# Moving R21's second-level differences one or two pairs earlier in both SwiGLUs of a macaron retention block

## The chip, the core and the metric

The kernel runs on one core of a Trainium2 chip. The metric is the time of one execution on the device, in microseconds (us), as the median of several runs; smaller is better. The engines are named as in the profile: PE is TensorE (matmuls), PEld its weight loads, DVE is VectorE, ACT is ScalarE, SP is SyncE, which issues the DMAs.

## The reference

One encoder layer over 1024 tokens of width 1024, in float32:

```python
h = h + 0.5 * swiglu_ffn(rmsnorm(h, norm_ffn1), ffn1_w_in, ffn1_w_out)
u = rmsnorm(h, norm_mix); proj = u @ w_in                 # q, k, v, gates, pool input
...                                                       # retention, pooling, gated merge
h = h + merged @ w_out
h = h + 0.5 * swiglu_ffn(rmsnorm(h, norm_ffn2), ffn2_w_in, ffn2_w_out)
return rmsnorm(h, norm_final)

def swiglu_ffn(x, w_in, w_out):                           # D_FF = 2816
    gate, up = jnp.split(x @ w_in, 2, axis=-1)
    return (jax.nn.silu(gate) * up) @ w_out
```

The case is about the two products `x @ w_in` (1024 x 1024 by 1024 x 5632), one in each SwiGLU.

## The kernel before, in words

**Three matmuls for one.** Every float32 operand is held as two halves, a rounded one and the rest. `split` makes them: ACT casts the first half (line 158), DVE subtracts to get the second (line 159). `mm3` (lines 178 to 180) then does three matmuls for each product of two blocks. The weights pass through `weights`, into a ring of five buffers (`wt`).

**Groups.** `w_in` is worked off in 22 groups, each of one 128-column tile of the gate and one of up. A group is one Strassen (Winograd) step over 2 x 2 blocks, with seven products, each of 12 matmuls of 128 x 512. `strassen` returns them as a list of steps (prepare, multiply): index 0 is P1 = L11 R11, 1 is P6 = S2 T2, 2 is P5 = S1 T1, 3 is P7 = S3 T3, 4 is P2 = L12 R21, 5 is P3 = S4 R22, 6 is P4 = L22 T4. L are weights; the S are sums of them, made by DVE for each group (lines 439, 452 and 456). R and T belong to the tokens and are made once for the whole SwiGLU, each in four tiles.

**Products in common.** `common(nx, A, B, n)` does P2 (n = 2) or P3 (n = 3) of two groups A and B together by a further Strassen step, in 42 matmuls of 128 x 256 instead of 24 of 128 x 512. It wants four differences of the token operand (y1 to y4 of R21 or of R22), which `Next.blocks` makes once, in six pieces of work: lines 356 (sums), 364 (differences), 158 and 159 (their splits). y1 is written over a block of the operand that the common product does not use, so from then on no plain P2 (or P3) may follow. A common product is three steps; its weights need one split of 128 x 512 and one of 128 x 256 more than the plain pair (`wx`, two `ws`, `wy`), and sums at lines 539, 540, 546 and 547; its results are put together by copies on ACT and additions on DVE (lines 573, 584, and 722 in `evac`).

**The order.** `pairs_of_both` yields the steps of a SwiGLU. The first two groups go plain (in SwiGLU 1 a third one, and ahead of them group 0 in another form). The others follow in pairs A, B, counted by k = 0, 1, ...: nine pairs in SwiGLU 1 and ten in SwiGLU 2. All of them have P3 in common. Pairs with k < `some` have P2 plain (steps A[4], B[4] right behind A[0], B[0]); with the last of them, k = `some` - 1, R21's differences are put on the queue. From k = `some` on P2 is in common: late in the pair for k = `some`, early in it after that. R22's differences are put on the queue with the last step ahead of the pairs, so that they are made in k = 0.

**The queue.** `Flow.run` prepares (`step[0]`) four steps ahead of the products (`step[1]`), and after each step's products takes one piece of work from a queue, first in, first out:

```python
            ahead.append(step)
            if len(ahead) > LOOK:
                done = ahead.popleft()
                if done is not None:
                    done[1]()
                    self.some(self.rate)
```

`rate` is 1 in both SwiGLUs. The end of a group puts four pieces there (line 736 or 739 multiplies the gate by the norm, ACT applies SiLU, line 742 twice multiplies gate and up), that of every second group four more (lines 755 to 767: operands for the second product, and their stores): 12 for a pair. Where a common product comes to its differences and they aren't made, `flow.until` takes from the queue until they are. What stands in the text in this way is the order of preference; a planner (Tile) that knows the dependences and a time for each instruction writes the final order of each engine's queue from it. Evacuations of PSUM are marked to go first (`soon`).

**Buffers.** The differences that stay live lie in tags `tl` (four buffers: three for R21, one for R22) and `t4` (nine: two for R22, one for the norm, six for the gate and up tiles). `c2` has eight buffers for sums and partial results.

Of the kernel before, what the change touches and what calls it, by code (L numbers as in the profile page):

```python
# [53 lines left out]
BY_OPERAND = (0, 4, 1, 3, 2, 6, 5)  # L54
# [36 lines left out]
def block_kernel(ctx: ExitStack, tc, x, x_tok, vecs, f1_in, f1_out, w_in, w_v, pool_w, w_ret, w_pool, w_o,  # L91
# [34 lines left out]
    def c2(name):  # L126
        return sb.tile([P, H], F32, tag="c2", bufs=N_C2, name=name)
# [8 lines left out]
    def load(dst, src):  # L136
        nc.sync.dma_start(dst, src)
# [8 lines left out]
    def half(t, j):  # L146
        return t[:, j * H : (j + 1) * H]
# [119 lines left out]
    class Next(Norm):  # L267
# [22 lines left out]
        def g(self, mt, v=None):  # L290
            if self.gain is None:
                return None
            v = vec if v is None else v
            return v[:, self.gain + mt : self.gain + mt + 1]
# [315 lines left out]
    def then(step, work):  # L610


        def body():
            step[1]()
            flow.add(*work)

        return step[0], body

    def pairs_of_both(nx, groups, first, some):

        groups = list(groups)
        A, B = (g(()) for g in groups[:2])
        steps = [g[m] for m in first for g in (A, B)]
        n = 2
        if len(groups) % 2:
            C = groups[n](())
            steps += [C[m] for m in BY_SUM]
            n += 1
        tl_, t4_ = ("tl", N_TL), ("t4", N_T4)

        steps[-1] = then(steps[-1], nx.blocks("R22", [t4_, tl_, t4_], True))
        yield from steps
        for k, n in enumerate(range(n, len(groups), 2)):
            A, B = (g((2, 3) if k >= some else (3,)) for g in groups[n : n + 2])
            yield A[0]
            yield B[0]
            if k < some:
                yield A[4]
                yield then(B[4], nx.blocks("R21", [tl_] * 3, True)) if k == some - 1 else B[4]
            elif k > some:  # L640
                yield from common(nx, A, B, 2)

            yield from (A[3], A[1], B[3], B[1], A[2], B[2])
            if k != some:
                yield from common(nx, A, B, 3)
                yield A[6]
                yield B[6]
            else:
                yield from common(nx, A, B, 2)
                yield A[6]  # L650
                yield B[6]
                yield from common(nx, A, B, 3)
# [49 lines left out]
    def ffn_in(nx, w, ops, name, start=None):  # L702

        R, T, B, T4 = ops
        hid = {}

        def group(g):
            gate_up = {}

            def dest(which):  # L710
                tile, j = which
                if tile not in gate_up:
                    gate_up[tile] = (tl if start and g == 0 else t4)(f"{name}{'gu'[tile]}{g}")
                return half(gate_up[tile], j)

            later = []

            def evac(which, in0, in1):
                tile, j = which
                dst, rms = dest(which), nx.rb  # L720
                if in1 is not None:
                    tt(dst, in0, in1, ADD)
                elif not tile and rms is not None:
                    tt(dst, in0, half(rms, j), MUL)
                    return
                else:
                    copy(dst, in0)
                if not tile:
                    later.append(j)

            def end():
                gate, up = gate_up[0], gate_up[1]

                def scale():
                    if len(later) == 2:
                        tt(gate, gate, nx.rms(), MUL)
                    else:
                        for j in later:
                            tt(half(gate, j), half(gate, j), half(nx.rms(), j), MUL)

                def times(j):
                    tt(half(up, j), half(gate, j), half(up, j), MUL)

                flow.add(scale, lambda: act(gate, gate, AF.Silu), lambda: times(0), lambda: times(1))
                hid[g] = up
                k = g % FH
                if g < FH:
                    return
                lo, hi, e = hid.pop(k), up, {}
                R11, R12, R21, R22 = half(lo, 0), half(lo, 1), half(hi, 0), half(hi, 1)  # L750

                def w1():

                    e["n"], e["m"] = gate, c2(f"{name}m{k}")
                    tt(half(e["n"], 0), R12, R11, SUB)

                def w1b():
                    tt(half(e["n"], 1), R22, R12, SUB)
                    load(B[k], e["n"])

                def w2():
                    tt(R12, R22, half(e["n"], 0), SUB)
                    load(R[k], lo)
                    load(T[k], hi)

                def w3():
                    tt(e["m"], R21, R12, SUB)
                    load(T4[k], e["m"])
                    done.add(k)

                flow.add(w1, w1b, w2, w3)

            if start and g == 0:
                return plain_group(nx, start, f"{name}{g}_", evac, end)
            return lambda shared: strassen(nx, w[g, 0], w[g, 1], f"{name}{g}_", evac, end, shared=shared, dest=dest)

        done = ops_done.setdefault(name, set())
        order = [g for k in range(FH) for g in (k, k + FH)]
        if start:

            return chain(group(0), pairs_of_both(nx, (group(g) for g in order[1:]), BY_OPERAND, 3))
        return pairs_of_both(nx, (group(g) for g in order), BY_OPERAND, 2)


    def plain_group(nx, blocks, name, evac, end):

        t, w = {}, {}

        def step(o, i, j):


            def prep():
                if j == 0:
                    w[o, i] = weights(blocks[2 * o + i], f"{name}w{o}{i}")

            def body():
                if i == 0:
                    t[o] = bank(f"{name}{o}{j}")
                for k in range(4):
                    mm3(t[o], parts(w[o, i], k), parts(nx.operand(("R11", "R12", "R21", "R22")[2 * i + j], k)),  # L800
                        i == 0 and k == 0, i == 1 and k == 3)
                if i == 1:
                    evac((o, j), t[o], None)
                    if (o, j) == (1, 1):
                        end()

            return prep, body

        return [step(o, i, j) for j in range(2) for i in range(2) for o in range(2)]
# [285 lines left out]
    def ffn1():  # L1095
        for n, step in enumerate(ffn_in(first, f1_in, ops1, "a", lead)):
            flow.rate = 1
            yield step
        flow.rate = 2
        yield from ffn_out(first, ops1, ops_done["a"], f1_out, x, "b", mix.quarter, end1)  # L1100
# [237 lines left out]
    order = [("q", 0), ("k", 0), *(o for pair in zip(heavy, light) for o in pair), *light[len(heavy) :]]  # L1338
# [482 lines left out]
    def second():  # L1821
        for n, step in enumerate(ffn_in(ffn2, f2_in, ops2, "c")):
            flow.rate = 1
            yield step
        flow.rate = 2
# [89 lines left out]
```

## Time and profile before

| | |
|---|---|
| median of 3 runs (lowest to highest) | 2153.55 us (2153.22 to 2153.73) |
| the profiled execution, its span | 2153.71 us, 2151.9 us |
| granted clock of TensorE | 1.000 |
| PE, PEld, DVE, ACT busy | 2136.8, 1814.0, 1884.0, 1110.4 us |
| SwiGLU 1's pairs, k = 0 to 8 | 87.7 to 424.0 us of the span |
| SwiGLU 2's pairs, k = 0 to 9 | from 1557.2 us of the span |

Rows of the windows view give a stretch, its length, and the busy time and number of instructions (in brackets) of PE, PEld, DVE, ACT and POOL in it, then the granted clock. Rows of the timeline give start, duration, engine, line, operation, output<-inputs, shape and count. A name such as `a_wS` is that of a tile with its numbers left out: a and c are SwiGLU 1 and 2, `a_wL` and `a_wS` are split weights of a plain product, `a_wx`, `a_ws`, `a_wy` those of a product in common, `n1x`, `n1R21y` and `n1R22y` belong to the differences.

### The profile page before, as it was taken

The numbers are of one execution on the slowest core, as the hardware profiler recorded it, in microseconds if no ns is written. First come the engines' busy times: TensorE is split into PE (matmuls) and PEld (weight loads), VectorE is DVE, ScalarE is ACT, GpSimd is POOL, SyncE is SP. The second block draws the span as 40 slices with busy tenths as digits, with TensorE's granted clock in tenths as the row PEclk, the third lists the DMA queues.
The fourth block names the chain that finished last, engine by engine and source line by source line (L and its number), as shares of the span: only waits on it lengthen the run. The fifth ranks groups of instructions, "written<-read, shape, count | busy, mean of one in ns | idle before, by whom it ended". The sixth has DMA issues, their size and how long they took to land.

```text
span 2151.9 us, 30188 instructions
## 1 busy us (share of the span) xinstructions
PE 2136.8 (99%) x10830; PEld 1814.0 (84%) x10830; DVE 1884.0 (88%) x3344; ACT 1110.4 (52%) x2102; POOL 0.2 (0%) x4
## 2 busy tenths in 40 slices
PE   9999999999999999999999999999999999999998
PEld 7888888888888888888888898888888888888887
DVE  8798888997987799999999877899988878899796
ACT  8544444454653544455457753446644544445454
POOL 0000000000000000000000000000000000000000
PEclk9999999999999999999999999999999999999999
DMA  7232423585537333232337567624133242358642
GB/s 255 77 133 74 136 85 128 180 288 183 178 119 245 109 110 123 101 131 105 119 109 242 179 225 251 219 92 162 64 104 116 74 136 85 127 181 292 197 130 100
DMA packets 120135, 320.96 MB, mean 149 GB/s; under 512 B 13232, under 2 KB 17456, under 8 KB 119984
## 3 DMA queue, kind: packets, MB, share of 16 engines
q1 hardware_dynamic: 119408, 317.98, 43.6%
q8 instruction: 85, 1.39, 0.3%
q10 hardware_dynamic: 576, 1.05, 0.1%
q14 instruction: 66, 0.54, 0.1%
HBM read 228.27 MB, written 90.70 MB: 148 GB/s over the span
## 4 chain that ended last, share of the span: by engine, by line
PE 83%; DVE 11%; DMA 2%; ACT 2%; issue 2%; SPq 0%; DVEq 0%; ACTq 0%
PE c_b L178 2%; PE c_b L179 2%; PE c_b L180 2%; PE a_b L178 2%; PE a_b L180 2%; PE a_b L179 2%; PE c_e L178 2%; PE c_e L179 2%; PE c_e L180 2%; PE a_e L179 2%; PE a_e L180 2%; PE a_e L178 2%; PE a_a L180 1%; PE a_a L179 1%; PE a_a L178 1%
## 5 line engine op out<-in xcount | busy, mean ns | idle before, releaser
L179 PE MATMUL c_b<-n3T,c_wS 128*128 128x512 f32 x176 | 68.5, 389 | 0.0
L180 PE MATMUL c_b<-n3T,c_wS 128*128 128x512 f32 x176 | 68.5, 389 | 0.0
L178 PE MATMUL c_b<-n3T,c_wS 128*128 128x512 f32 x176 | 68.2, 389 | 0.0
L178 PE MATMUL a_b<-n1T,a_wS 128*128 128x512 f32 x168 | 65.4, 389 | 0.0
L179 PE MATMUL a_b<-n1T,a_wS 128*128 128x512 f32 x168 | 65.4, 389 | 0.0
L180 PE MATMUL a_b<-n1T,a_wS 128*128 128x512 f32 x168 | 65.3, 389 | 0.0
L179 PE MATMUL a_a<-n1R,a_wL 128*128 128x512 f32 x120 | 46.7, 389 | 0.0
L180 PE MATMUL a_a<-n1R,a_wL 128*128 128x512 f32 x120 | 46.7, 389 | 0.0
L178 PE MATMUL a_a<-n1R,a_wL 128*128 128x512 f32 x120 | 46.7, 389 | 0.0
L179 PE MATMUL c_a<-n3R,c_wL 128*128 128x512 f32 x112 | 43.7, 390 | 0.0
L180 PE MATMUL c_a<-n3R,c_wL 128*128 128x512 f32 x112 | 43.6, 389 | 0.0
L178 PE MATMUL c_a<-n3R,c_wL 128*128 128x512 f32 x112 | 43.6, 389 | 0.0
L178 PEld LDWEIGHTS c_b<-n3T,c_wS 128*128 128x128 f32 x176 | 33.0, 188 | 6.9
L180 PEld LDWEIGHTS c_b<-n3T,c_wS 128*128 128x128 f32 x176 | 33.0, 188 | 6.8
L179 PEld LDWEIGHTS c_b<-n3T,c_wS 128*128 128x128 f32 x176 | 33.0, 188 | 6.8
L179 PEld LDWEIGHTS a_b<-n1T,a_wS 128*128 128x128 f32 x168 | 31.5, 188 | 6.6
L180 PEld LDWEIGHTS a_b<-n1T,a_wS 128*128 128x128 f32 x168 | 31.5, 188 | 6.5
L178 PEld LDWEIGHTS a_b<-n1T,a_wS 128*128 128x128 f32 x168 | 31.5, 188 | 6.5
L159 DVE TENSOR_TENSOR a_wS<-a_S,a_wS 128x512 fp32r<-128x512 f32 x45 | 30.8, 685 | 6.8 <-ACT a_wS L158 6.8
L159 DVE TENSOR_TENSOR c_wS<-c_S,c_wS 128x512 fp32r<-128x512 f32 x46 | 31.5, 684 | 3.7 <-ACT c_wS L158 3.6
L179 PE MATMUL c_e<-n3T,c_wL 128*128 128x512 f32 x88 | 34.4, 391 | 0.0
L178 PE MATMUL c_e<-n3T,c_wS 128*128 128x512 f32 x88 | 34.4, 391 | 0.0
(3380 smaller groups left out, 8178.7 us busy)
## 6 DMA issues: line engine op xcount, KB each, us to landing
c_ra<-in_f_in SPq DMA_DIRECT2D x22, 512.0 KB, 3.7
c_rb<-in_f_in SPq DMA_DIRECT2D x22, 512.0 KB, 4.3
a_ra<-in_f_in SPq DMA_DIRECT2D x21, 512.0 KB, 3.7
a_rb<-in_f_in SPq DMA_DIRECT2D x21, 512.0 KB, 4.3
t<-au SPq DMA_DIRECT2D x11, 512.0 KB, 4.1
b<-ag SPq DMA_DIRECT2D x11, 512.0 KB, 3.5
r<-au SPq DMA_DIRECT2D x11, 512.0 KB, 3.6
br<-r SPq DMA_DIRECT2D x11, 512.0 KB, 5.2
```

The source lines that it names most:

```text
L159: tt(lo, src, hi.bitcast(F32), SUB)
L178: mm(dst, w[0], m[0], start=start, stop=False, skip_group_check=True)
L179: mm(dst, w[0], m[1], start=False, stop=False, skip_group_check=True)
L180: mm(dst, w[1], m[0], start=False, stop=stop, skip_group_check=True)
```

## The change

`pairs_of_both` gets `some` = 1 from both callers, instead of 3 in SwiGLU 1 and 2 in SwiGLU 2. With that R21's differences are put on the queue in k = 0, behind B[4] of that pair, and P2 is in common in k = 1 to 8 of SwiGLU 1 (it was 3 to 8) and in k = 1 to 9 of SwiGLU 2 (it was 2 to 9). Nothing else differs.

```diff
         if start:
 
-            return chain(group(0), pairs_of_both(nx, (group(g) for g in order[1:]), BY_OPERAND, 3))
-        return pairs_of_both(nx, (group(g) for g in order), BY_OPERAND, 2)
+            return chain(group(0), pairs_of_both(nx, (group(g) for g in order[1:]), BY_OPERAND, 1))
+        return pairs_of_both(nx, (group(g) for g in order), BY_OPERAND, 1)
```

## The prediction

> **What bounds the kernel now.** I read the page's busy times and its chain first, then the windows view over single pairs, then the timeline of DVE and PE at the pairs that the change touches.
>
> ```profile
> PE 2136.8 (99%) x10830; PEld 1814.0 (84%) x10830; DVE 1884.0 (88%) x3344; ACT 1110.4 (52%) x2102; POOL 0.2 (0%) x4
> PE 83%; DVE 11%; DMA 2%; ACT 2%; issue 2%; SPq 0%; DVEq 0%; ACTq 0%
> ```
>
> PE is busy for 2136.8 of 2151.9 us and carries 83% of the chain. So a matmul less is time less, and anything else costs only where PE is left without weights. DVE, second with 88%, is the engine that can do that: every product needs a split of its weights, which DVE ends. I call reserve the time from the end of that split to the product's first matmul; as long as it is positive, PE doesn't wait.
>
> The pairs, each from the first matmul of A[0] to that of the next pair's (SwiGLU 1: k = 2, k = 3, k = 4 to 8; SwiGLU 2: k = 1, k = 2):
>
> ```profile
> 163.49:200.94 37.45, 37.45 (x187) 31.82 (x186) 30.64 (x58) 15.36 (x29) 0.00 (x0) 1.00 0.30 106
> 200.94:237.99 37.05, 37.05 (x205) 32.27 (x204) 34.06 (x67) 19.56 (x36) 0.00 (x0) 1.00 0.34 107
> 237.99:424.03 186.04, 185.63 (x1022) 161.25 (x1021) 160.75 (x284) 89.21 (x166) 0.00 (x0) 1.00 0.37 126
> ...
> 1595.34:1632.81 37.47, 37.47 (x188) 31.82 (x187) 34.72 (x65) 17.05 (x32) 0.00 (x0) 1.00 0.30 106
> 1632.81:1669.82 37.01, 37.01 (x205) 32.26 (x204) 33.98 (x67) 19.55 (x36) 0.00 (x0) 1.00 0.32 107
> ...
> 168.93:174.37 5.44, 5.44 (x25) 4.51 (x24) 5.44 (x10) 1.73 (x3) 0.00 (x0) 1.00 0.74 288
> 243.47:248.25 4.78, 4.78 (x43) 4.77 (x42) 4.78 (x9) 4.07 (x8) 0.00 (x0) 1.00 0.00 0
> 88.53:146.00 57.47, 57.43 (x272) 47.62 (x272) 56.94 (x102) 30.41 (x53) 0.00 (x0) 1.00 0.37 129
> 1580.00:1613.80 33.80, 33.75 (x169) 28.29 (x168) 33.00 (x64) 16.56 (x32) 0.00 (x0) 1.00 0.26 84
> ```
>
> PE has no gap in any of them. A pair with P2 plain takes 37.45 or 37.47 us, one with P2 in common 37.05 or 37.01, the later ones 186.04 / 5 = 37.21. The sixth and seventh rows are a plain P2 of two groups (24 matmuls, 5.44 us) and one in common (42, 4.78 us). The last two rows are where the change lands: from before k = 0 until well into k = 1 DVE is full, 56.94 of 57.47 us in SwiGLU 1 and 33.00 of 33.80 in SwiGLU 2. There R22's differences are already being made.
>
> **The change part by part.** *Products.* Three pairs get P2 in common: k = 1 and 2 of SwiGLU 1, k = 1 of SwiGLU 2. PE alone would save 5.44 - 4.78 = 0.66 us for each. The pairs of before show less, since something small comes back in waits. For the form that k = 1 gets, 37.45 - 37.05 = 0.40 and 37.47 - 37.01 = 0.46; for that of k = 2, 37.45 - 37.21 = 0.24. Sum -1.1 us; bounds -2.0 (all of it) and 0.
>
> The Trainium skill has a rule against this ("TensorE: Matmul & The Clock Gate", section "Back-to-back issue gap"): sustained pairs of weight load and matmul are spaced about 131 ns at 512 columns and 81 ns at 128, so narrow matmuls pay for more than their columns. With 98 ns at 256 columns, an estimate between those two, three products in common would lose 3 x (42 x 98 - 24 x 131) = 2.9 us instead of saving. The sixth and seventh rows contradict it, with 5.44 / 24 = 227 ns and 4.78 / 42 = 114 ns, so the sum goes by them.
>
> *DVE's work.* Prices are the pitch at which DVE takes instructions in a run:
>
> ```profile
> 1560.28 1.89 DVE L742 TENSOR_TENSOR cu<-cg,cu 128x512 f32<-128x512 f32 x3
> 118.05 0.75 DVE L159 TENSOR_TENSOR n1R22y<-n1x,n1R22y 128x256 fp32r<-128x256 f32 x2
> 90.27 2.35 DVE L736 TENSOR_TENSOR ag<-ag,n1rb 128x1024 f32<-128x1024 f32 x2
> L356 DVE TENSOR_TENSOR n1x<-n1R 128x512 f32<-128x512 f32 x8 | 5.5, 684 | 0.0
> L159 DVE TENSOR_TENSOR n1R21y<-n1x,n1R21y 128x256 fp32r<-128x256 f32 x6 | 2.5, 419 | 0.0
> ```
>
> Three at 128 x 512 take 1.89 us and one 0.684, so the pitch is 0.60; at 128 x 256 it is 0.75 - 0.419 = 0.33, and at 128 x 1024 about 2.35 / 2 = 1.17. R21's differences are half of the eight sums shown (R22 has the other half), eight differences and eight splits: 4 x 0.60 + 16 x 0.33 = 7.7 us in six pieces of 1.86, 0.66, 1.32, 1.86, 0.66 and 1.32. They exist before too, in k = 2 and k = 1, where no row above shows PE waiting, so nothing is gained by their going. A P2 in common costs DVE three splits of 0.60 and one of 0.33, six narrow sums (2.0), two wide ones (1.2) and two multiplications of 1.17: 7.7 us. Plain it is two splits, two evacuations and two multiplications of 0.60: 3.6. So 4.1 us more for each of the three pairs. Its added casts and copies are ACT's, which is busy for about half of every row above; no DMA is added, and SP's and POOL's queues carry the same.
>
> *Place 1: the first products of k = 1.* In order, R21's six pieces are taken behind the three steps of P3 in common of k = 0, then behind A[6], B[6] and A[0] of k = 1: just after R22's, with DVE full. Preparing runs four steps ahead, so the first four pieces, 5.7 us, stand ahead of the weights of A[1] of k = 1, and the first five, 6.4, ahead of those of B[3]. The 12 pieces of the pair before slide back behind them. And A[4], B[4] of k = 1, two long products that are cheap for DVE, are gone from in between, so that A[3] and what follows is wanted 5.44 us earlier. SwiGLU 1, then SwiGLU 2, around A[1] and B[3] of k = 1:
>
> ```profile
> 127.94 0.68 DVE L159 TENSOR_TENSOR a_wL<-a_ra,a_wL 128x512 fp32r<-128x512 f32 x1
> ...
> 129.48 0.68 DVE L739 TENSOR_TENSOR ag<-ag,n1rb 128x512 f32<-128x512 f32 x1
> 130.08 0.68 DVE L159 TENSOR_TENSOR a_wL<-a_ra,a_wL 128x512 fp32r<-128x512 f32 x1
> ...
> 131.29 0.69 DVE L742 TENSOR_TENSOR au<-ag,au 128x512 f32<-128x512 f32 x1
> ...
> 132.50 0.69 DVE L742 TENSOR_TENSOR au<-ag,au 128x512 f32<-128x512 f32 x1
> ...
> 133.70 0.68 DVE L159 TENSOR_TENSOR a_wS<-a_S,a_wS 128x512 fp32r<-128x512 f32 x1
> 139.57 0.39 PE L178 MATMUL a_b<-n1T,a_wS 128*128 128x512 f32 x1
> 1604.93 0.69 DVE L159 TENSOR_TENSOR c_wS<-c_rb,c_wS 128x512 fp32r<-128x512 f32 x1
> 1611.68 0.39 PE L178 MATMUL c_e<-n3T,c_wS 128*128 128x512 f32 x1
> ```
>
> SwiGLU 1, A[1]: the split ends at 134.38, PE comes at 139.57, reserve 5.2. PE would come 5.44 earlier; DVE has 5.7 more ahead, less the splits of A[4], B[4] (1.2) and the multiplications at 129.48, 131.29 and 132.50 that slide back (1.8): 5.2 - 5.44 - 2.7 = -2.9. SwiGLU 2, B[3]: reserve 1611.68 - 1605.62 = 6.1; less 5.44; 6.4 more ahead, less 1.2, four multiplications (2.4) and one evacuation of A[4] (0.6), so 2.2: -1.5. The other steps between are less negative by the same count. So PE waits 2.9 + 1.5 = 4.4 us in all. DVE being full in those rows, work put ahead delays what follows by its full length, unless the planner puts a sum for a later step behind it: one such sum (0.60) for each place is the nearest thing in those rows. I take 4.4, and keep 0 and 7 as bounds (a reserve off by 2 us either way).
>
> *Place 2: the products in common that follow.* In k = 1 and k = 2 three common products come with only A[6], B[6] and A[0], B[0] between them. SwiGLU 1 before has this at k = 3 and 4, from A[6] of k = 3 to A[3] of k = 4:
>
> ```profile
> 223.56 0.69 DVE L159 TENSOR_TENSOR a_wL<-a_rb,a_wL 128x512 fp32r<-128x512 f32 x1
> 225.67 0.69 DVE L159 TENSOR_TENSOR a_wL<-a_rb,a_wL 128x512 fp32r<-128x512 f32 x1 [1.42 <-ACT a_wL L158]
> 227.57 0.39 PE L178 MATMUL a_e<-n1T,a_wL 128*128 128x512 f32 x1
> 244.86 0.68 DVE L159 TENSOR_TENSOR a_wS<-a_rb,a_wS 128x512 fp32r<-128x512 f32 x1
> 248.25 0.40 PE L178 MATMUL a_e<-n1T,a_wS 128*128 128x512 f32 x1
> ```
>
> The reserve is 227.57 - 224.25 = 3.3 at the first and 248.25 - 245.54 = 2.7 at the second, and DVE idles for 1.42 us between, so at the first it isn't DVE that holds it down. Place 1 ends with no reserve at B[3]. From there to the common P2, PE has four products, 4 x 2.72 = 10.9 us, and DVE 8.6: splits and sums for B[1], A[2], B[2] (3.6) and the first step of P2 (1.9), R21's last piece (1.3) and three multiplications (1.8). So about 2 us are back, of which the rows take 0.6 away by A[3]. What is left is within the error of my counts: I put 0.5 us of waiting for each SwiGLU, 1.0 in all; bounds 0 and 2 x 2.7.
>
> *Sum.* -1.1 + 4.4 + 1.0 = +4.3 us on the profiled execution's 2153.71, that is 2158.0; it stands 0.16 above the median of the runs, inside their spread of 0.5. I say 2158.0.
>
> **The rivals.** *The reserve suffices.* Not slower: the planner knows DVE's backlog and may put R21's pieces into the gaps that remain, or leave the 12 pieces of the pair before for later. For it: in k = 2 and k = 1 before, the same six pieces cost PE nothing. Against: there the reserve had been filled before, here R22's pieces have just emptied it. It decides at a reserve 2.9 and 1.5 us larger than I count. Then only the products are left: 2153.55 - 1.1 = 2152.4. *In between*, with place 1 at half: about 2155.5.
>
> *Buffers instead of DVE.* Gate and up have six `t4` tiles, three groups. With the 12 pieces six steps later, the tiles of k = 0 come free later, and common P2 of k = 1 needs its two gate tiles then. If each waits for the pieces that free it, two or three steps of 2.72 us (12 matmuls at 227 ns) are lost in each SwiGLU on top: 2158.0 + 8 = 2166. Against it: k = 3 of before has the same order and the same six pieces ahead, and no gap (37.05 us, all busy).
>
> *It changes nothing else.* With `some` = 1, k = 0 still has its plain P2 ahead of the differences, and the common one follows in k = 1, so the change does what it says; that it would not has no chance worth a number. Nor do I see how it could gain over 2.0 us plus the 0.4 us that PE idles in the third row.
>
> **How the numbers follow.** Waits at place 1 about as counted or worse: 0.55; of this about 0.45 lies above +4.3 us, which is 0.2%, about what a measurement of this kernel can tell from no change, and 0.10 just below. In between: 0.18. Reserve suffices: 0.18. Buffers: 0.05. Unknown gains over 0.2%: 0.04. So slower 0.45 + 0.05 = 0.50, same 0.10 + 0.18 + 0.18 = 0.46, faster 0.04. The range for 8 in 10 goes from the case without waits, 2152.3, to place 1 at 7 with part of place 2: 2153.55 - 1.1 + 7 + 3 = 2162.5. Within the likeliest case alone it is 2156 to 2162.5.
>
> **What would show it.** Right: PE has 54 matmuls more (18 for each pair); in the timeline, gaps of PE behind DVE's splits of `a_wS` and `c_wS` in A[3], A[1], B[3] of k = 1, 2 to 4 us in SwiGLU 1 and 1 to 2 in SwiGLU 2; k = 1 longer than 37.5 us, k = 3 of SwiGLU 1 near 37; DVE full from 88 us until past 160 us. Wrong: k = 1 at 37.0 us without gaps (the planner hid it), or waits of ACT's copies or DVE's additions on freed tiles, or a difference that comes up outside the two stretches.

## The result, and the profile after

| | before | changed |
|---|---|---|
| median (lowest to highest) of 14 runs each | 2153.45 us (2151.5 to 2154.89) | 2157.64 us (2154.89 to 2160.94) |
| the profiled execution, its span | 2153.71, 2151.9 us | 2157.64, 2155.8 us |
| PE's instructions | 10830 | 10884 |

The ratio is 1.0023, with a 95% interval of 1.0016 to 1.0030: the change makes the kernel 0.23% slower, 4.2 us. 2158.0 us was forecast.

First the busy times and the shares of the chain on the page of the changed kernel:

```profile
PE 2139.9 (99%) x10884; PEld 1816.4 (84%) x10884; DVE 1895.0 (88%) x3368; ACT 1115.1 (52%) x2117; POOL 0.2 (0%) x4
PE 90%; DVE 6%; DMA 1%; ACT 1%; issue 1%; SPq 0%; DVEq 0%; ACTq 0%
```

There are 54 more matmuls, 18 for each of three pairs, so the change does what it says. DVE's share of the chain fell from 11% to 6% although, as the rows further down show, it is DVE that made PE wait. The shares of the chain don't find 4 us in 2156.

The windows view does. It shows the changed kernel in the three pairs k = 0, 1 and 2 (from A[0] of k = 0 to A[0] of k = 3) of SwiGLU 1 and of SwiGLU 2, then k = 3 of SwiGLU 1, and last 3.4 us in k = 1 of SwiGLU 1:

```profile
86.82:202.88 116.06, 114.52 (x595) 97.26 (x594) 110.40 (x206) 59.96 (x112) 0.00 (x0) 0.99 0.34 118
1559.77:1673.67 113.90, 113.24 (x596) 96.02 (x594) 103.58 (x198) 55.87 (x107) 0.00 (x0) 1.00 0.32 104
202.88:240.04 37.16, 37.16 (x205) 32.26 (x204) 31.54 (x57) 17.37 (x32) 0.00 (x0) 1.00 0.32 107
129.10:132.50 3.40, 3.40 (x10) 2.63 (x9) 2.70 (x6) 1.50 (x4) 0.00 (x0) 0.50 0.00 0
```

The same three pairs of before:

```profile
87.67:200.94 113.27, 113.23 (x559) 95.48 (x558) 101.00 (x182) 54.08 (x97) 0.00 (x0) 1.00 0.34 121
1557.23:1669.82 112.59, 112.54 (x577) 95.95 (x576) 100.33 (x192) 54.27 (x101) 0.00 (x0) 1.00 0.31 106
```

The three pairs take 116.06 - 113.27 = 2.79 us more in SwiGLU 1 and 113.90 - 112.59 = 1.31 us more in SwiGLU 2, together 4.1 of the measured 4.2 us. PE was busy for all but 0.04 us of the first stretch before; now it is idle for 116.06 - 114.52 = 1.54 us, and its granted clock there is 0.99 instead of 1.00. k = 3 of SwiGLU 1 takes 37.16 us, which is what such a pair took before (37.05 to 37.21 us). The timeline of PE in the changed kernel, at A[0] of k = 1 of SwiGLU 1 and at A[3] and A[1] of k = 1 of SwiGLU 2:

```profile
125.99 0.28 PE L180 MATMUL a_b<-n1R22y,a_wy 128*128 128x256 f32 x1
127.77 0.50 PE L180 MATMUL a_a<-n1R,a_wL 128*128 128x512 f32 x1 [1.50 <-DVE a_wL L159]
...
129.05 0.61 PE L179 MATMUL a_a<-n1R,a_wL 128*128 128x512 f32 x1
129.46 0.63 PE L180 MATMUL a_a<-n1R,a_wL 128*128 128x512 f32 x1
129.89 0.63 PE L178 MATMUL a_a<-n1R,a_wL 128*128 128x512 f32 x1
...
1603.68 0.40 PE L179 MATMUL c_e<-n3T,c_wS 128*128 128x512 f32 x1
1604.23 0.50 PE L180 MATMUL c_e<-n3T,c_wS 128*128 128x512 f32 x1
...
1607.15 0.39 PE L179 MATMUL c_b<-n3T,c_wS 128*128 128x512 f32 x1
1607.98 0.50 PE L180 MATMUL c_b<-n3T,c_wS 128*128 128x512 f32 x1 [0.43 <-DVE c_wS L159]
```

In SwiGLU 1 PE stands for 127.77 - 125.99 - 0.11 = 1.67 us (a matmul of 256 columns takes 0.11 us) behind DVE's split of `a_wL`. A little more than 1 us later its matmuls start 0.41 to 0.43 us apart instead of 0.23: the clock is at half, 0.50 in the row from 129.10 us. In SwiGLU 2 there are small waits for the weights `c_wS`, the longest 1607.98 - 1607.15 - 0.23 = 0.60 us behind DVE's split at A[1]; by the starts of the matmuls those at A[3] and A[1] add up to 1.7 us.

Next DVE's own rows around the split that PE waits for in SwiGLU 1 (line 159, `a_wL`), first before, with the first matmul of A[0], then changed:

```profile
122.53 0.69 DVE L159 TENSOR_TENSOR a_wL<-a_ra,a_wL 128x512 fp32r<-128x512 f32 x1
123.14 0.76 DVE L159 TENSOR_TENSOR n1R22y<-n1x,n1R22y 128x256 fp32r<-128x256 f32 x2
...
124.65 0.40 PE L178 MATMUL a_a<-n1R,a_wL 128*128 128x512 f32 x1
...
127.00 0.68 DVE L159 TENSOR_TENSOR a_wL<-a_ra,a_wL 128x512 fp32r<-128x512 f32 x1
```

```profile
121.67 0.69 DVE L356 TENSOR_TENSOR n1x<-n1R 128x512 f32<-128x512 f32 x1
122.28 0.75 DVE L159 TENSOR_TENSOR n1R22y<-n1x,n1R22y 128x256 fp32r<-128x256 f32 x2
122.95 0.42 DVE L364 TENSOR_TENSOR n1x<-n1x 128x256 f32<-128x256 f32 x1
...
126.10 0.41 DVE L159 TENSOR_TENSOR n1R<-n1x,n1R 128x256 fp32r<-128x256 f32 x1
126.43 0.68 DVE L722 TENSOR_TENSOR ag<-a_b,ag 128x512 f32<-128x512 f32 x1
127.03 0.68 DVE L159 TENSOR_TENSOR a_wL<-a_ra,a_wL 128x512 fp32r<-128x512 f32 x1
```

Counted from the start of k = 0, A[0]'s split comes at 122.53 - 87.67 = 34.9 us before and at 127.03 - 86.82 = 40.2 us now, 5.3 us later. R21's first operations stand ahead of it: two sums (119.13 and 121.67), one difference (122.95), one split (126.10), 1.9 us. Most of the remainder is older work that came behind the split before and comes ahead of it now: the rest of R22's differences (1.3 us) and five evacuations (lines 573, 584, 722; 2.5 us). A sum of line 439 (0.6 us) went the other way, so this makes 3.2 us. DVE's short waits are the rest.

### The profile page after: what moved, and what is told of

It is laid out like the page before. It is cut to its first block, busy times and chain, and to the rows that moved or that the text cites. A ratio compares the mean times of both kernels' runs of the same rounds, so it can differ in the third digit from the quotient of the medians.

```text
span 2155.8 us, 30360 instructions
## 1 busy us (share of the span) xinstructions
PE 2139.9 (99%) x10884; PEld 1816.4 (84%) x10884; DVE 1895.0 (88%) x3368; ACT 1115.1 (52%) x2117; POOL 0.2 (0%) x4
## 4 chain that ended last, share of the span: by engine, by line
PE 90%; DVE 6%; DMA 1%; ACT 1%; issue 1%; SPq 0%; DVEq 0%; ACTq 0%
PE c_b L180 2%; PE c_b L178 2%; PE c_b L179 2%; PE a_b L178 2%; PE a_b L180 2%; PE a_b L179 2%; PE a_e L179 2%; PE a_e L178 2%; PE a_e L180 2%; PE c_e L178 2%; PE c_e L179 2%; PE c_e L180 2%; PE a_a L180 1%; PE a_a L179 1%; PE a_a L178 1%; PE bp6b L180 1%
## 5 line engine op out<-in xcount | busy, mean ns | idle before, releaser
L180 PE MATMUL a_a<-n1R,a_wL 128*128 128x512 f32 x104 | 41.1, 397 | 1.5 <-DVE a_wL L159 1.5
L179 PE MATMUL a_a<-n1R,a_wL 128*128 128x512 f32 x104 | 41.2, 396 | 0.0
L178 PE MATMUL a_a<-n1R,a_wL 128*128 128x512 f32 x104 | 41.0, 394 | 0.0
L179 PE MATMUL c_a<-n3R,c_wL 128*128 128x512 f32 x104 | 40.6, 390 | 0.0
L178 PE MATMUL c_a<-n3R,c_wL 128*128 128x512 f32 x104 | 40.5, 389 | 0.0
L180 PE MATMUL c_a<-n3R,c_wL 128*128 128x512 f32 x104 | 40.5, 389 | 0.0
L178 PE MATMUL c_e<-n3T,c_wS 128*128 128x512 f32 x88 | 34.6, 393 | 0.0
L180 PE MATMUL c_e<-n3T,c_wS 128*128 128x512 f32 x88 | 34.3, 390 | 0.1
```

What stands on the lines that cost most here:

```text
L178: mm(dst, w[0], m[0], start=start, stop=False, skip_group_check=True)
L179: mm(dst, w[0], m[1], start=False, stop=False, skip_group_check=True)
L180: mm(dst, w[1], m[0], start=False, stop=stop, skip_group_check=True)
```

## The experiments

Two theories stood against each other after this. **Backlog:** P2 in common gains a little by itself, and all of the loss is DVE's, which gets R21's differences while it is still behind with R22's. **Cover:** the loss comes with the plain P2 that k = 1 no longer has, long products on PE that cost DVE little. A third, **buffers**, was the prediction's rival.

### e1_dummy: the work without the products in common

The kernel before, with six pieces of the same cost put on the queue in k = 0, their results going to spare tiles; P2 stays plain in k = 1.

```diff
...
-                yield then(B[4], nx.blocks("R21", [tl_] * 3, True)) if k == some - 1 else B[4]
+                if k in (0, some - 1):
+                    yield then(B[4], nx.blocks("R21", [tl_] * 3, True, k != some - 1))
+                else:
+                    yield B[4]
```

> The kernel before, with six pieces of work more in k = 0 of each SwiGLU that cost DVE and ACT what R21's differences cost; their output goes to spare tiles and is not used. P2 stays plain in k = 1, and the real differences stay where they were. Backlog theory (the differences' DVE work right behind R22's empties the reserve): A[0] and B[0] of k = 1 come ahead of the plain P2, so SwiGLU 1 still loses about 3.3 us there; in SwiGLU 2 the wait was at A[3] and A[1], which stand behind the plain P2 again, so about 0. Sum about +3 us. Cover theory (what hurts is that the plain P2, long for PE and cheap for DVE, is gone from k = 1): 0. Buffer theory (gate and up tiles come free six steps later): as the changed kernel, +4, with waits of ACT's copies or DVE's additions on freed tiles.

Measured: 2155.83 us, ratio 1.0021 (1.0011 to 1.0030). The windows view of the three pairs, in SwiGLU 1 and 2:

```profile
88.80:203.89 115.09, 113.55 (x559) 95.34 (x558) 108.30 (x202) 57.17 (x106) 0.00 (x0) 1.00 0.34 119
1558.19:1672.50 114.31, 113.45 (x577) 95.58 (x576) 107.09 (x210) 56.54 (x109) 0.00 (x0) 1.00 0.30 104
```

and its timeline of PE at A[0] of k = 1 of SwiGLU 1 and at B[3] of k = 1 of SwiGLU 2:

```profile
129.76 0.50 PE L180 MATMUL a_a<-n1R,a_wL 128*128 128x512 f32 x1 [1.50 <-DVE a_wL L159]
...
1614.16 0.50 PE L180 MATMUL c_e<-n3T,c_wS 128*128 128x512 f32 x1 [0.42 <-DVE c_wS L159]
```

The pairs take 1.82 and 1.72 us more than before, and the wait at A[0] of SwiGLU 1 is there again, 1.67 us. So work for DVE at this place makes PE wait, without any further product in common. It isn't a mere move here: the real pieces stay where they were, and DVE is busy for 7.3 and 6.8 us longer than before. The sum came near the +3 us expected, the division did not: SwiGLU 1 was to lose 3.3 us, and SwiGLU 2 was to be free, since the two plain products were to cover for 5.4 us. There the waits for `c_wS` at A[3] and B[3] make 1.3 us, and 0.6 us comes at the P2 in common of k = 2. So this count of the cover is wrong, and no run says why.

### e2_nodve: the products in common without the work

The changed kernel without DVE's part of R21's differences.

```diff
+                if R == "R21" and self.name in ("n1", "n3"):
...
+                    for h in range(2):
+                        copy(m[:, h, at], src[:, h, HI].bitcast(F32))
...
+                    return
```

> The changed kernel without DVE's part in R21's differences: no sums, no differences, no splits; ACT copies six narrow blocks twice into the tiles of y2, y3 and y4 (12 copies in place of 8 casts), the queue has its six pieces as before, and the products in common run on these other numbers. Left out: the values of R21's differences. Backlog theory: no waits of PE on split weights in k = 1 of either SwiGLU, only the products saved, about -1 us against the kernel before (2152.4), 5 us under the changed one. Cover theory: as the changed kernel, +4. Buffer theory: the 12 pieces of the pair before still slide back by six steps, so as the changed kernel, +4.

Measured: 2151.66 us, ratio 0.9999 (0.9991 to 1.0008). The windows view of the three pairs:

```profile
87.35:199.52 112.17, 112.13 (x595) 96.28 (x594) 103.07 (x186) 60.49 (x116) 0.00 (x0) 1.00 0.35 122
1554.80:1666.89 112.09, 112.01 (x596) 96.28 (x594) 96.22 (x178) 56.07 (x111) 0.00 (x0) 1.00 0.31 106
```

All matmuls of the change are in, and k = 1 has no wait behind a split: 1.10 and 0.50 us less than before. So the products in common gain 1.6 us without that work, and with DVE's part away neither the lost cover nor the tiles that come free later cost anything. With e1_dummy this settles for backlog: the loss is in DVE's part of six pieces. The whole time can't show 1.6 us: a ratio of 0.9993 lies inside the interval.

### e4_mid: one pair later in SwiGLU 1

The changed kernel with `some` = 2 in both SwiGLUs; SwiGLU 2 is then as before.

```diff
-            return chain(group(0), pairs_of_both(nx, (group(g) for g in order[1:]), BY_OPERAND, 1))
-        return pairs_of_both(nx, (group(g) for g in order), BY_OPERAND, 1)
+            return chain(group(0), pairs_of_both(nx, (group(g) for g in order[1:]), BY_OPERAND, 2))
+        return pairs_of_both(nx, (group(g) for g in order), BY_OPERAND, 2)
```

> The kernel before with the differences of SwiGLU 1 made in k = 1 instead of k = 2 (SwiGLU 2 as before): one pair more with P2 in common. Backlog theory: R22's pieces are a whole pair past and DVE has caught up, so no waits; only 0.2 to 0.5 us gained, no difference that the times can show. Cover and buffer theory: k = 2 of SwiGLU 1 then stands as k = 1 of the changed kernel does, which loses 3 us: +2 to +3.

Measured: 2151.70 us, ratio 1.0002 (0.9994 to 1.0011). The three pairs of SwiGLU 1:

```profile
87.35:200.12 112.77, 112.73 (x577) 95.85 (x576) 106.78 (x200) 58.26 (x106) 0.00 (x0) 1.00 0.34 122
```

It takes 0.50 us less than before, without a wait behind a split: the same pieces cost nothing there in k = 1, when R22's have been made. In SwiGLU 1 the loss comes only with k = 0. Later, in k = 4, PE waits for 1.16 us at a product in common, for an addition of DVE (line 573). Such a wait stands in other pairs of other kernels too (0.28 us in k = 6 of the kernel before, 1.65 us in k = 7 of SwiGLU 2 in e2_nodve), so nothing here ties it to the move.

### e3_front: R21's pieces at the head of the queue

The changed kernel, but R21's six pieces go ahead of what already waits in the queue.

```diff
...
+            step[1]()
+            flow.back.extendleft(reversed(work))
...
-                yield then(B[4], nx.blocks("R21", [tl_] * 3, True)) if k == some - 1 else B[4]
+                yield ahead(B[4], nx.blocks("R21", [tl_] * 3, True)) if k == some - 1 else B[4]
```

> The changed kernel, with R21's six pieces put at the head of the queue instead of its end, so that DVE gets them six steps earlier, during A[3] to B[2] of k = 0. Backlog theory: in SwiGLU 2 DVE has some 6 us idle there (busy 6.2 of 12 us in k = 0 of the kernel before), so its waits go, and k = 0 and 1 together take about 1.5 us less than in the changed kernel; in SwiGLU 1 DVE is full from before k = 0 on, so nothing is gained there, and as all six pieces now stand ahead of A[0] it may lose up to 2 us more. Sum between +2 and +5 against the kernel before. Cover theory: no difference from the changed kernel in either. Buffer theory: the pieces that free the tiles come six steps later already in k = 0, so more waits in both.

Measured: 2158.04 us, ratio 1.0032 (1.0020 to 1.0044). The windows view of the three pairs of both SwiGLUs, and of 6 us of SwiGLU 1:

```profile
87.41:206.10 118.69, 116.16 (x596) 99.06 (x594) 109.28 (x205) 59.70 (x112) 0.00 (x0) 0.97 0.33 116
1562.60:1675.51 112.91, 112.39 (x596) 96.01 (x594) 103.52 (x198) 56.35 (x107) 0.00 (x0) 1.00 0.31 105
128.00:134.00 6.00, 5.66 (x21) 4.79 (x20) 4.44 (x11) 1.46 (x4) 0.00 (x0) 0.50 0.00 0
```

and its timeline of PE in k = 0 of SwiGLU 1:

```profile
125.64 0.39 PE L178 MATMUL a_x<-n1R22y,a_ws 128*128 128x256 f32 x1 [0.78 <-ACT n1R22y L158]
```

In SwiGLU 2 the loss falls from 1.31 to 0.32 us, as the backlog theory wants of pieces that are done sooner. In SwiGLU 1 it grows from 2.79 to 5.42 us: now PE waits for R22's own differences in the P3 in common of k = 0, and the clock falls to 0.50 behind these waits. There the pieces, coming sooner, push aside what is due first. Together the pairs lose 5.7 us and the median 6.5, where +2 to +5 was expected.

### e5_late and e9_half: six, then three steps later

The changed kernel with empty pieces ahead of R21's six, so that each is taken that many steps later: six in e5_late, three in e9_half.

```diff
-                yield then(B[4], nx.blocks("R21", [tl_] * 3, True)) if k == some - 1 else B[4]
+                yield then(B[4], [lambda: None] * 6 + nx.blocks("R21", [tl_] * 3, True)) if k == some - 1 else B[4]
```

> The changed kernel, with six empty pieces put on the queue ahead of R21's six, so that these are taken behind B[0] to A[2] of k = 1 instead of behind P3 in common of k = 0 to A[0] of k = 1; P2 is in common from k = 1 on as in the changed kernel. Backlog theory: nothing stands ahead of the first weights of k = 1 but R22's pieces, as in the kernel before; by the count of the prediction the reserve at A[1] is 5.2 - 5.44 + 1.2 + 1.8 = 2.8 us, at A[3] about 1.8, so no waits of PE on split weights in k = 1 of either SwiGLU. Their stretches from k = 0 to k = 1 take 3.6 us (SwiGLU 1) and 1.6 us (SwiGLU 2) less than in the changed kernel; against the kernel before about -1 us. A wait of up to 1 us may come at P2 in common of k = 1, which needs the differences two steps after the last piece. Buffer theory: the pieces that free the tiles slide back by six steps more, so longer waits than in the changed kernel. Cover theory: as the changed kernel, +4.

e5_late, measured: 2158.57 us, ratio 1.0031 (1.0021 to 1.0041); 1 us less than before was expected, so this missed. The windows view of the three pairs:

```profile
87.42:203.17 115.75, 112.76 (x596) 96.52 (x594) 110.05 (x206) 59.38 (x112) 0.00 (x0) 1.00 0.33 116
1561.02:1674.33 113.31, 112.70 (x595) 96.52 (x594) 103.25 (x198) 55.41 (x107) 0.00 (x0) 1.00 0.30 103
```

and the timeline of all engines in SwiGLU 1, at B[2] of k = 1, which the planner put inside P2 in common, and at A[0] of k = 2:

```profile
147.28 0.50 PE L178 MATMUL a_b<-n1T,a_wS 128*128 128x512 f32 x1 [0.49 <-ACT a_v L481]
...
163.61 0.69 DVE L762 TENSOR_TENSOR au<-au,ag 128x512 f32<-128x512 f32 x1
...
164.33 0.65 ACT L566 COPY ag<-a_y 128x256 f32<-128x256 f32 x2 [1.38 <-DVE au L762]
...
164.75 0.50 PE L178 MATMUL a_a<-n1R,a_wL 128*128 128x512 f32 x1 [2.46 <-ACT ag L566]
```

No split makes PE wait in A[0] to B[3] of k = 1 any more. Instead, in k = 2, ACT waits for DVE's line 762, which is one of the 12 pieces of k = 0 and frees a gate tile; PE waits for ACT's copy out of PSUM, 2.46 us. Before that, PE waits for 0.49 us at B[2] of k = 1, for another copy of ACT. The longer wait is the rival "buffers", which the changed kernel itself doesn't show: six steps more of delay bring it about.

> The changed kernel with three empty pieces ahead of R21's six, half of what the late kernel has. Backlog and buffers together, as the runs so far show them: only the first piece stands ahead of the weights of A[1] of k = 1 and the first two ahead of B[3]'s, so by the count the reserve is about 0.9 us at A[1] and 1 us at B[3]: no waits on split weights in k = 1, or under 0.5 us. The 12 pieces that free gate and up tiles slide back by nine steps; with six no wait on a freed tile came, with twelve one of 2.5 us in SwiGLU 1, so here between 0 and 1 us. First two pairs: about 75.5 us in SwiGLU 1 (kernel before 75.8, changed 78.9) and 75.2 in SwiGLU 2 (75.6, 76.7); the time within 1 us of the kernel before. If the waits on split weights stay, the backlog theory is wrong on when the work has to come.

e9_half, measured: 2153.57 us, ratio 1.0009 (1.0000 to 1.0018). The windows view of the three pairs:

```profile
87.61:200.92 113.31, 113.00 (x596) 96.45 (x594) 110.58 (x207) 60.01 (x113) 0.00 (x0) 1.00 0.34 121
1557.15:1669.58 112.43, 112.38 (x595) 96.43 (x594) 103.86 (x199) 55.97 (x108) 0.00 (x0) 1.00 0.30 106
```

and in its timeline the one place in k = 1 of SwiGLU 1 where PE waits for a split, at the P2 in common:

```profile
146.99 0.38 PE L180 MATMUL a_y<-n1R,a_ws 128*128 128x256 f32 x1 [0.28 <-DVE a_ws L159]
```

DVE does the same work as in the changed kernel, 110.58 against 110.40 us in SwiGLU 1, three steps later, and the loss of 2.79 and 1.31 us is gone: +0.04 and -0.16 against before. So what costs is when the pieces come. It isn't faster than the kernel before: against e2_nodve the pairs still take 1.14 and 0.34 us more, of which about 0.5 us lies at the product of the last row. Its median is 1.75 us above that of the kernel before, measured beside it, where at most 1 us was expected.

### e6_pool: R21's differences on GpSimd

The changed kernel with R21's sums, differences and second halves on GpSimd (POOL).

```diff
...
-                    tt(v, m[:, 0].bitcast(F32), m[:, 1].bitcast(F32), ADD)
+                    on = nc.gpsimd.tensor_tensor if R == "R21" and self.name in ("n1", "n3") else tt
+                    on(v, m[:, 0].bitcast(F32), m[:, 1].bitcast(F32), ADD)
...
```

> The changed kernel, with R21's sums, differences and the second halves of their splits on GpSimd, which is idle, instead of DVE (same numbers). Backlog theory: DVE has 7.7 us less to do, so no waits on split weights at A[0] to B[3] of k = 1, about -1 us against the kernel before, unless GpSimd slows DVE down while it works or is so slow that P2 in common of k = 1 waits for the differences: GpSimd has some 30 us for 20 instructions, so it may take 1.5 us for each. Cover and buffer theory: as the changed kernel, +4.

Measured: 2180.01 us, ratio 1.0126 (1.0110 to 1.0141). The windows view of the three pairs, then the group of POOL's sums in SwiGLU 2 (busy us, mean ns), then three rows of DVE's timeline in SwiGLU 1 (the edit shifts line numbers: 356 is 357 here, 722 is 725, and the splits of differences are at 377):

```profile
86.64:212.72 126.08, 117.34 (x595) 98.58 (x594) 107.93 (x186) 59.84 (x112) 22.81 (x20) 0.96 0.31 109
1570.87:1697.07 126.20, 117.14 (x595) 98.69 (x594) 105.39 (x178) 55.36 (x107) 19.55 (x20) 0.96 0.28 94
```

```profile
L357 POOL TENSOR_TENSOR n3x<-n3R 128x512 f32<-128x512 f32 x4 | 5.8, 1452 | 1461.4 <-DVE c_wy L159 1458.1 <-DVE cu L725 2.2 <-DVE n3R22y L377 1.0
```

```profile
123.78 1.00 DVE L377 TENSOR_TENSOR n1R<-n1x,n1R 128x256 fp32r<-128x256 f32 x1 [3.01 <-ACT n1R L376]
...
126.99 1.22 DVE L159 TENSOR_TENSOR a_wL<-a_ra,a_wL 128x512 fp32r<-128x512 f32 x1
...
133.17 0.68 DVE L725 TENSOR_TENSOR ag<-a_b,ag 128x512 f32<-128x512 f32 x1
```

12.8 and 13.6 us are lost. POOL takes 1.45 us for a sum that DVE makes in 0.684, and beside it DVE's own instructions with both inputs in SBUF, where tiles lie, take 1.22 us instead of 0.69 (128 x 512) and 1.00 instead of 0.42 (128 x 256), some still longer. An evacuation, which has one input in PSUM, where PE's results come out, keeps its 0.68 us (last row). DVE has 20 instructions less, and the slower ones eat up most or all of what that saves: it is busy for 107.93 us against 110.40 in SwiGLU 1 of the changed kernel, and for 105.39 against 103.58 in SwiGLU 2. So this run could not test the backlog theory: it puts another loss in its place.

### e7_again and e8_again: the changed kernel twice more

The kernel is unchanged; the question was whether the half clock belongs to the change.

> The changed kernel once more, for its profile. Its first profile shows a wait of 1.67 us at A[0] of k = 1 in SwiGLU 1 and then matmuls of B[0] at twice the spacing, with a granted clock of 0.50 from 130 to 132 us. If DVE's splits set the pace up to A[1], as the backlog theory has it, A[1] starts at the same distance from k = 0 (50 us) whether or not the clock falls: without the fall the 1.6 us show as waits at A[3] and A[1]. If the slower clock is a loss of its own, A[1] comes 1.6 us earlier without it.

> As the run before: the changed kernel a third time, for one more sample of the clock after the wait.

Measured: 2154.50 and 2157.46 us, one execution each. The windows view of e7_again, three pairs of SwiGLU 1 and of SwiGLU 2, and of 2 us behind the wait at A[0]:

```profile
86.95:202.02 115.07, 113.10 (x595) 96.12 (x594) 110.50 (x206) 60.43 (x113) 0.00 (x0) 1.00 0.34 119
1556.97:1670.86 113.89, 113.23 (x596) 96.08 (x594) 103.60 (x198) 55.83 (x107) 0.00 (x0) 1.00 0.31 104
130.00:132.00 2.00, 2.00 (x10) 1.65 (x10) 2.00 (x6) 1.50 (x3) 0.00 (x0) 1.00 0.00 0
```

and its timeline of PE at A[0] and A[1] of k = 1 of SwiGLU 1:

```profile
127.89 0.50 PE L180 MATMUL a_a<-n1R,a_wL 128*128 128x512 f32 x1 [1.51 <-DVE a_wL L159]
...
136.33 0.50 PE L180 MATMUL a_b<-n1T,a_wS 128*128 128x512 f32 x1 [0.42 <-DVE a_wS L159]
```

The same rows of e8_again, SwiGLU 1 and the 2 us:

```profile
87.31:203.84 116.53, 114.81 (x596) 97.40 (x594) 110.31 (x206) 60.04 (x112) 0.00 (x0) 0.99 0.34 118
130.00:132.00 2.00, 2.00 (x6) 1.56 (x5) 2.00 (x5) 0.29 (x1) 0.00 (x0) 0.50 0.00 0
```

The wait at A[0] is 1.68 us in the one and 1.69 us in the other, and the clock behind it is 1.00 in the one and 0.50 in the other. With the first profile of the changed kernel (half) and e1_dummy (full, after 1.67 us) it fell in 2 of 4. A[1] starts 136.79 - 86.82 = 49.97 us behind the start of k = 0 in the first profile and 135.28 - 86.95 = 48.33 us in e7_again, so the slower clock is a loss of its own. It costs 116.06 - 115.07 = 1.0 us or 116.53 - 115.07 = 1.5 us. Eight matmuls take 0.20 us longer each, 1.6 us, but DVE's splits run on meanwhile, and of the wait that e7_again has at A[1], about 0.6 us, less is left.

## Why the prediction was right, and where it was not

The sum was +4.3 us, 2.8 in SwiGLU 1 and 1.5 in SwiGLU 2; the stretches show +2.79 and +1.31, the medians +4.2. Step by step:

- **Products.** Forecast -1.1 us (-0.64 and -0.46), measured in e2_nodve -1.10 and -0.50. The term of SwiGLU 1 was sized too small: 0.55 for each pair there, where 0.40 and 0.24 were taken from whole pairs in which a common product gives something back. e4_mid has 0.50 for one pair.
- **Place 1.** The mechanism was right, shown by e1_dummy, e2_nodve and e9_half together. What the changed kernel takes beyond e2_nodve holds place 2 as well, for which, together, 2.9 + 0.5 = 3.4 us in SwiGLU 1 and 1.5 + 0.5 = 2.0 in SwiGLU 2 were forecast. In SwiGLU 1 it is 115.07 - 112.17 = 2.9 us where the clock stayed and 116.06 - 112.17 = 3.9 or 116.53 - 112.17 = 4.4 us where it fell, in SwiGLU 2 113.90 - 112.09 = 1.8 us.
- **Where in place 1.** This step failed. The first and largest wait came at A[0], which the count left out; it had said A[1], with "the other steps between" less negative. R21's first piece (two sums, a difference and a split, 1.86 us) is taken behind the first step of P3 in common, and A[0] is prepared after that, so it stands ahead of A[0]'s weights in the order of the queue too. The reserve there was 1.43 us before (the split ends at 122.53 + 0.69 = 123.22, PE comes at 124.65), so by the prediction's own count this piece makes a wait of 0.4 us. What took it to 1.67 us is the 3.2 us of older work that the planner put ahead of the split as well: the prediction took the order of the queue for the order of DVE. Why the planner chose so no run shows. The delay found at A[0] makes that at A[1] smaller (0.1 us in the first profile, 0.6 in e7_again). In SwiGLU 2 the waits were at A[3] and A[1], not at B[3].
- **Place 2.** Forecast 0.5 us for each SwiGLU, measured about 0.25 us by the starts of PE's matmuls at the P2 in common of k = 2: nearer the lower bound.
- **The clock, and luck.** The prediction had no loss by the clock. In e7_again, where the clock stayed, the three pairs take 115.07 - 113.27 = 1.80 and 113.89 - 112.59 = 1.30 us more than before, 3.1 us in all. So the sum of 4.3 us was about 1 us too much in SwiGLU 1, and the half clock brought about 1 us that was not in it. That the two meet is luck.
- **A reading.** The prediction says that PE has no gap in any of its rows of pairs. In the third it idles for 186.04 - 185.63 = 0.41 us, which is 0.08 us of the 37.21 us for each of its five pairs.
- **Rivals.** "The reserve suffices" fell in both SwiGLUs, "buffers" too; e9_half and e5_late show what each looks like when the same pieces come three and six steps later.

**Open.** The whole times of the experiments lie up to 3 us above what the three pairs say (e5_late +6.0 against +3.2 us; e9_half +1.7 against -0.1). The stretch between the SwiGLUs, in which no kernel here differs, takes from 1131.5 us (e1_dummy) to 1135.2 us (e6_pool) in the profiles, so one profile for each kernel can't divide such a remainder.

## What to carry to other kernels

An engine that is off the critical path for most of the span can still be the one without slack in the stretch where work is moved: count its backlog there, from the rows of that stretch, and not its share of the whole. If moved work costs although its amount is the same, shift it by a few steps before giving it up: here three steps later took 4 us of loss in the pairs away and six brought another wait. And where a planner orders the queues, the size of a delay can be counted from the work, but its place has to be read from the trace.

## What was not expected of the hardware

A wait of PE of 1.7 us was enough to halve its clock in two of four executions, for 3.4 us (129.1 to 132.5 us in the changed kernel), and not in the other two; the wait of 2.46 us in e5_late left it at 1.00. In e3_front it was at 0.50 for 6.8 us (127.3 to 134.1 us). The Trainium skill ("TensorE: Matmul & The Clock Gate", section "What's actually happening") has the array fall to half its clock after at least one idle window of some 3.4 us, with windows that run freely. The trace agrees on the half (0.50 granted), and its lengths are one and two such windows; but here a wait of half a window was enough. Whether the place of the wait in such a window decides, no run shows.

Beside GpSimd's instructions, most of DVE's with both inputs in SBUF took nearly twice their time or more (0.69 to 1.22 us for 128 x 512, up to 1.77 us), while its evacuations of PSUM kept theirs. So work given to GpSimd was not taken off DVE.
